# Moving the gates' scratch off the complex scan's buffer, and one product per scan step instead of two

## Chip, cores and metric

The kernel runs on one core of a Trainium2 chip. A core has five engines that matter here: PE (TensorE, matrix multiplications), DVE (VectorE), ACT (ScalarE), POOL (GpSimd) and SP (SyncE, which issues the transfers). Each engine takes its own instructions strictly in the order of its queue, and waits for the others through semaphores. The metric is the device time of one execution in microseconds (us); lower is better.

## What the kernel computes

One layer of a hybrid encoder on 1024 positions of width 1024 in float32: four token mixers in parallel (gated DeltaNet, S5, RG-LRU, a short gated convolution), then cross-attention, then a gated feed-forward part. Two pieces matter. The S5 mixer runs a complex linear recurrence in both directions:

```
h_t = a_t h_{t-1} + b_t
a2r * b1r - a2i * b1i + b2r,   a2r * b1i + a2i * b1r + b2i
```

The gated DeltaNet needs, for every head and position, a gate and a decay, which are small:

```
beta  = sigmoid(beta_logit)
log_a = -exp(a_log) * softplus(alpha + dt_bias)
gam   = cumsum(log_a)            # within chunks
```

## The kernel before

All large products run on PE, each as three products of split float32 parts (`mm3`, L158). PE's instructions stand exactly in the order in which the program is written; the instructions of DVE, ACT, POOL and SP are put in order by a scheduler when the program is built, from its own guess of the times. That order is then fixed.

While the S5 mixer's other work goes on, PE is kept busy by `fill(n)`, which takes the next `n` pieces from a list of projections: a few gate tiles, and then four pairs of RG-LRU and short convolution (`lru`, `short_conv`).

The stage around the change runs like this, all in `tile_trunk` (L1936 to L1951):

- `s5_in` computes the inputs of the recurrence into the buffer `H`. Its last instructions on DVE are the copies at L598.
- `Scalars.run` computes the gates and decays. PE multiplies by a 16-column weight (`mm3` at L764) and transposes the result (L770). Then comes a chain of some seventy small DVE operations of 8 or 64 elements in each of the 128 partitions (`softplus`, `exact_exp`, each operation needs the one before it), with a power taken on POOL in its middle (L721). The result `g` goes back to PE for four small products (L788, L789), which PE issues at a fixed place in its order. DVE picks them up at L792.
- `s5_scan` runs the recurrence on DVE alone: 7 steps of 16 x 64 elements, 15 steps of 64 elements, 7 steps of 15 x 64 elements. A step is `turn` (two cross products into `t1`, one product into `t0`, their sum in `t0`) and an addition into `H`.
- `s5_out`, eight times, reads `H` for the outputs, with `fill(12)` in between. Its first PE instructions need the scan to be done.

The small operations take their scratch from boxes of 1024 columns, in the order in which they ask for it; the first two boxes hold `tri` (L756) and `row` (L765), and everything behind them falls into the third:

```
def part(w):
    if not at or at[-1] + w > S:
        at.append(0)
        self.box = self.big(boxes[len(at) - 1])
...
for go in sc.run(hh, hl, s.parts("xc", "gl", "cm0")):
...
t0, t1 = [self.big(f"cm{i}").rearrange("p (a n) -> p a n", a=16) for i in range(2)]
```

A name such as `cm0` is one buffer. Whoever asks for it again gets it when its last reader is done. The scan's `t0` is `cm0` too. `L` is used by `s5_in` before and by `s5_out` after.

Of the kernel before, what the change touches and what calls it, by code (L numbers as in the profile page):

```python
# [24 lines left out]
ADD, SUB, MUL, MAX, MIN = ALU.add, ALU.subtract, ALU.mult, ALU.max, ALU.min  # L25
# [292 lines left out]
class SPhase:  # L318
# [305 lines left out]
    def s5_scan(self):  # L624

        K = self.K
        H = self.H.rearrange("p (a k) n -> p a k n", k=8)
        t0, t1 = [self.big(f"cm{i}").rearrange("p (a n) -> p a n", a=16) for i in range(2)]

        def turn(out, a, x):  # L630
            n = x.shape[1]
            ri = lambda y: y.rearrange("p n (r g) -> p n r g", r=2)
            b = lambda y: y.unsqueeze(1).to_broadcast([P, n, 64])
            for r in range(2):
                y = slice(32 * r, 32 * r + 32), slice(32 - 32 * r, 64 - 32 * r)
                K.tt(t1[:, :n, y[0]], b(a[1])[:, :, y[0]], x[:, :, y[1]], MUL)
            K.tt(out[:, :n], b(a[0]), x, MUL)
            K.tt(out[:, :n], out[:, :n], t1[:, :n], ADD)

        for k in range(1, 8):  # L640
            turn(t0, self.a8, H[:, :, k - 1])
            K.tt(H[:, :, k], H[:, :, k], t0, ADD)
            yield
        for a in range(1, 16):
            turn(t0, self.a64, H[:, a - 1:a, 7])
            K.tt(H[:, a:a + 1, 7], H[:, a:a + 1, 7], t0[:, 0:1], ADD)
            if a % 5 == 0:
                yield
        for k in range(7):
            turn(t0, self.a8, t0[:, 0:15] if k else H[:, 0:15, 7])  # L650
            K.tt(H[:, 1:16, k], H[:, 1:16, k], t0[:, 0:15], ADD)
            yield
# [539 lines left out]
def gate_tile(K, pool, i, hh, hl):  # L1192
    ps = yield from K.proj(K.a["wi"][GT + i], hh, hl)
    t = pool.tile([P, S], F32, name="tho")
    K.nc.scalar.activation(t, ps, AF.Tanh, scale=0.5)
    K.nc.sync.dma_start(K.th[i], t)
    yield False
# [32 lines left out]
def mem_kv(K, norm):  # L1230

    nc, tc, a = K.nc, K.tc, K.a
    M = 256
    K.kvd = K.dram.tile([16, P, M], F32, name="kvd")
    with tc.tile_pool(name="kv", bufs=1) as p, tc.tile_pool(name="kvr", bufs=2) as r, \
            tc.tile_pool(name="kvw", bufs=5) as w:
        x = p.tile([P, KD, M], F32, name="mx")
        ready = [f() for f in K.weights(a["wkv"][0], pool=w)]
        for k in range(0, KD, 2):
            nc.sync.dma_start(x[:, k:k + 2], a["mem"][:, k:k + 2])  # L1240
        hm = p.tile([P, 2, KD, M], F32R, name="hm")
        acc, row, late = [], None, []
        for k in range(KD):
            K.gained(r, x[:, k], k, "xamn", hm[:, 0], hm[:, 1], acc)
        rr = K.rrow(r, p, acc[0], M)
        steps = (1, 5, 8)
        for i in range(16):
            ps = K.sm.tile([P, 512], F32, name="sm")[:, :M]
            parts = K.weights(a["wkv"][i], pool=w) if i else [lambda x=x: x for x in ready]
            g = K.mm3(ps, parts, hm[:, 0], hm[:, 1], n=M)  # L1250
            if i in (1, 2):
                for _ in range(18):
                    next(g)
                row = next(rr)
            if i in steps:
                next(norm)
            K.run(g)
            late.append((i, ps))
            while late and row is not None:
                j, ps = late.pop(0)  # L1260
                t = r.tile([P, M], F32, name="kvt")
                K.tt(t, ps, row, MUL)
                nc.sync.dma_start(K.kvd[j], t)
# [636 lines left out]
@with_exitstack  # L1900
def tile_trunk(ctx, tc, a, out):
    ctx.enter_context(tc.manual_schedule(engines={mybir.EngineType.PE}))
    K = _K(ctx, tc, a)
    nc = tc.nc
    big = ctx.enter_context(tc.tile_pool(name="big", bufs=1))
    h = big.tile([P, 2, KD, S], F32R, name="big")
    hh, hl = h[:, 0], h[:, 1]
    with tc.tile_pool(name="xin", bufs=2) as xp:
        X = xp.tile([P, KD, S], F32, name="X", bufs=1)

        def norm():
            acc = []
            for k in range(KD):
                nc.sync.dma_start(X[:, k], a["x"][:, k])
                K.sumsq(xp, X[:, k], S, acc)
            yield
            yield from K.normed(xp, lambda k: X[:, k], acc[0], "mixn", hh, hl)

        mem_kv(K, norm())
    K.lo = "dve"  # L1920
    fill = Fill()
    with tc.tile_pool(name="tho", bufs=1, side="right") as tp, ExitStack() as gs:
        gates = [gate_tile(K, tp, i, hh, hl) for i in range(32)]
        sc = Scalars(K, gs)
        with ExitStack() as c:
            s = SPhase(K, c, hh, hl, fill)
            fill.add(*gates[:5])
            for j in range(4):
                fill.add(s.pair(j))
            fill.add(*gates[5:6])  # L1930
            s.s5_prep()
            s.s5_c()
            s.lru_prep()
            for j in range(4):
                s.s5_u(j)
            s.s5_in()  # L1936
            waits = [12, 12, 46, 0]
            scan = s.s5_scan()
            for go in sc.run(hh, hl, s.parts("xc", "gl", "cm0")):
                if not go:  # L1940
                    fill(waits.pop(0))
            K.lo = "pool"
            for _ in scan:
                fill(16)
            fill(12)
            for o in range(8):
                s.s5_out(o)
                fill(12)
            fill(48)
            s.s5_glu()  # L1950
            fill.drain()  # L1951
        K.lo = "pool"
        fill.add(*gates[6:])
        with ExitStack() as c:
            g = GPhase(K, c, hh, hl, fill, sc)
            g.heads()
            fill.drain()
    mg = branches(K, big)
    x1d = K.dram.tile([KD, P, S], F32, name="x1d")
    with tc.tile_pool(name="keep", bufs=1, side="right") as keep, tc.tile_pool(name="bq", bufs=1) as bq:  # L1960
        rcol = keep.tile([P, 8], F32, name="rcol")
        with tc.tile_pool(name="at", bufs=1) as at:
            with tc.tile_pool(name="xr", bufs=1) as xr:
                hx = Quarters(bq)
                kT = at.tile([P, 2, KD, 256], F32R, name="kT")
                vt = at.tile([P, 2, 2, D], F32R, name="vt")
                mem = memory(K, at, kT, vt)
                acc = []
                with tc.tile_pool(name="x1", bufs=1) as xp:
                    for j in range(KD):  # L1970
                        x = xp.tile([P, S], F32, name="X")
                        nc.sync.dma_start(x, a["x"][:, j])
                        ps = K.run(K.proj(a["wmo"][j], mg[:, 0], mg[:, 1]))
                        K.tt(x, x, ps, ADD)
                        for h in range(2):
                            K.scaled(x[:, 512 * h:512 * h + 512], j, "xan", hx.at(0, j, h), hx.at(1, j, h))
                        K.sumsq(xr, x, S, acc)
                        nc.sync.dma_start(x1d[j], x)
                        next(mem)
                qt = big.tile([P, 2, KD, S], F32R, name="big")  # L1980
                es = {}
                rrow = queries(K, xr, hx, qt, acc[0],
                               lambda: es.update({n: scores(K, at, qt, kT, n) for n in range(AHEAD)}), keep, rcol)
            with tc.tile_pool(name="att", bufs=1) as p:
                ot = Quarters(bq)
                tail = Tail(K, tc, bq, keep, rrow, rcol, x1d, out)
                attend(K, p, at, qt, ot, kT, vt, es, tail.ahead)
        tail.run(big, ot)
# [16 lines left out]
```

## Time and profile before

| what | value |
|---|---|
| median of 3 runs | 2454.89 us (2451.81 to 2455.99) |
| the profiled execution, its own time | 2456.03 us |
| its span in the trace | 2454.2 us |
| PE busy | 2360.2 us, 96% of the span |
| DVE busy | 1495.9 us, 61% |
| ACT busy | 927.5 us, 38% |
| POOL busy | 898.4 us, 37% |
| mean granted share of PE's clock | 0.983 |

Busy time is the time in which an engine executes something. An engine that is rarely busy can still set the end, where the busiest one waits for it. The granted clock is the share of PE's full 2.4 GHz that it was given; 0.5 is the lower level of 1.2 GHz.

### The profile page before, as it was taken

To read this page: it belongs to the slowest core of one execution; us is meant where nothing else is said; L and a number is where in the kernel's file an instruction comes from. 1 tells how busy PE (TensorE), PEld (TensorE's weight loads), DVE (VectorE), ACT (ScalarE), POOL (GpSimd) and SP (SyncE) were. 2 spreads that over 40 slices of the span, in tenths; PEclk is the share of its full clock that TensorE was granted. 3 is DMA by queue.
4 is the path that set the end of the run, shared out by engine and by line. 5 is a ranking of instruction groups with operands and counts; after the bars stand their busy time and mean duration, and the time that the engine had idled before them with its cause. 6 is when DMAs were issued, how large, how long until landed. Compare 5 with 4: busy or idle time off the path is not lost. (4 is left out here: it accounts for less than half of the span.)

```text
span 2454.2 us, 31835 instructions
## 1 busy us (share of the span) xinstructions
PE 2360.2 (96%) x11495; PEld 1920.8 (78%) x11495; DVE 1495.9 (61%) x2983; ACT 927.5 (38%) x1461; POOL 898.4 (37%) x644
## 2 busy tenths in 40 slices
PE   7999998899999999999999999999899999999997
PEld 6777767778877787787778888888688888888886
DVE  6883998855947848569345543275766666663421
ACT  6372444634323233232222133255444444453431
POOL 6422224435324233232122222204344444564543
PEclk8999998999999999999899999999999999999998
DMA  7443112342111211112165444105322222255541
GB/s 260 118 109 98 39 65 74 106 146 75 65 48 48 69 48 57 61 53 69 40 235 176 146 153 136 48 5 177 124 77 78 78 78 78 94 180 161 193 157 63
DMA packets 136206, 250.45 MB, mean 102 GB/s; under 512 B 15344, under 2 KB 42992, under 8 KB 135920
## 3 DMA queue, kind: packets, MB, share of 16 engines
q1 hardware_dynamic: 136048, 248.41, 31.2%
q8 instruction: 91, 1.49, 0.2%
q14 instruction: 67, 0.55, 0.1%
HBM read 188.58 MB, written 57.67 MB: 100 GB/s over the span
## 5 line engine op out<-in xcount | busy, mean ns | idle before, releaser
L142 POOL TENSOR_TENSOR wl<-wr,wh 128x512 fp32r<-128x512 f32 (+1 forms) x507 | 695.0, 1380 | 1308.7 <-ACT wh L140 1151.5
L171 PE MATMUL pp<-big,wh 128*128 128x512 f32 x2560 | 729.9, 403 | 16.0 <-DVE sa L192 12.3
L140 ACT ACTIVATE wh<-wr 128x512 fp32r<-128x512 f32 (+1 forms) x526 | 320.2, 621 | 977.2 <-PE pp L171 515.0
L171 PEld LDWEIGHTS pp<-big,wh 128*128 128x128 f32 x2560 | 475.1, 191 | 118.1 <-DVE sa L192 14.6
L171 PE MATMUL pp<-big,wl 128*128 128x512 f32 x1280 | 407.4, 400 | 0.0
L1483 PE MATMUL sm<-big,wh 128*128 128x512 f32 x1096 | 343.8, 395 | 6.0 <-ACT p L1702 4.4
L1483 PE MATMUL sm<-bigq,wh 128*128 128x512 f32 x1008 | 315.6, 394 | 0.7 <-ACT u L1706 0.7
L171 PEld LDWEIGHTS pp<-big,wl 128*128 128x128 f32 x1280 | 238.2, 191 | 47.9
L1483 PEld LDWEIGHTS sm<-big,wh 128*128 128x128 f32 x1096 | 206.3, 188 | 54.2 <-ACT p L1702 4.8
L1483 PEld LDWEIGHTS sm<-bigq,wh 128*128 128x128 f32 x1008 | 189.0, 188 | 45.1 <-ACT u L1706 1.1
L1483 PE MATMUL sm<-big,wl 128*128 128x512 f32 x548 | 214.8, 392 | 0.0
L1483 PE MATMUL sm<-bigq,wl 128*128 128x512 f32 x504 | 197.1, 391 | 0.0
L171 PE MATMUL pp<-yhl,wh 128*128 128x512 f32 x512 | 137.5, 390 | 2.1 <-DVE acc L189 0.8
L1483 PEld LDWEIGHTS sm<-big,wl 128*128 128x128 f32 x548 | 103.4, 189 | 23.2
L189 DVE SCALAR_TENSOR_TENSOR pp<-ut,vec,pp 128x1023 f32<-128x1023 f32 x88 | 113.2, 1286 | 3.5 <-ACT pp L1760 0.4
L171 PEld LDWEIGHTS pp<-yhl,wh 128*128 128x128 f32 x512 | 95.9, 188 | 23.0 <-DVE acc L189 1.2
L1483 PEld LDWEIGHTS sm<-bigq,wl 128*128 128x128 f32 x504 | 94.7, 188 | 21.2
L192 DVE TENSOR_TENSOR t<-rb,x 128x8 f32<-128x8 f32 (+30 forms) x248 | 81.4, 366 | 0.0
L171 PE MATMUL pp<-yhl,wl 128*128 128x512 f32 x256 | 79.0, 390 | 0.0
L192 DVE TENSOR_TENSOR y<-y,t 128x8 f32<-128x8 f32 (+30 forms) x248 | 72.3, 330 | 0.0
L1760 ACT ACTIVATE pp<-ut,vec 128x1024 f32<-128x1024 f32 x44 | 53.1, 1207 | 46.5 <-DVE ut L192 46.5
L171 PE MATMUL pp<-bigq,wh 128*128 128x512 f32 x256 | 69.0, 392 | 0.0
(428 smaller groups left out, 3349.6 us busy)
## 6 DMA issues: line engine op xcount, KB each, us to landing
wr<-in_wi SPq DMA_DIRECT2D x144, 256.0 KB, 2.7
wr<-in_wup SPq DMA_DIRECT2D x88, 256.0 KB, 4.2
wr<-in_wdn SPq DMA_DIRECT2D x80, 256.0 KB, 3.9
thd<-tho SPq DMA_DIRECT2D x32, 512.0 KB, 2.9
thi<-thd SPq DMA_DIRECT2D x32, 512.0 KB, 4.1
gd<-sg SPq DMA_DIRECT2D x22, 512.0 KB, 2.9
gr<-gd SPq DMA_DIRECT2D x44, 256.0 KB, 4.1
wr<-in_wkv SPq DMA_DIRECT2D x32, 256.0 KB, 3.6
```

Of the source, the lines that this page charges most:

```text
L140: self.nc.scalar.activation(hi, src, AF.Copy)
L142: e.tensor_tensor(lo, src, hi.bitcast(F32), SUB)
L171: self.nc.tensor.matmul(ps[:, o:o + step], w[:, i], r[:, k, o:o + step], start=first, stop=last)
L189: self.nc.vector.scalar_tensor_tensor(out, in0, s, in1, op0, op1)
L192: (eng or self.nc.vector).tensor_tensor(out, a, b, op)
L1483: self.K.nc.tensor.matmul(ps, a[:, i], b, start=start and i == 0 and j == 0, stop=last and stop is not False, skip_group_check=stop is Non ...
L1760: K.nc.scalar.activation(c[b], t[b], AF.Identity, bias=K.v("fconvb", n), scale=K.v("fconv", 3 * n + 1))
```

## The change

Two edits. The third box of the small operations is `L` in place of `cm0`. And the two cross products of a scan step, each over half of the 64 columns, become one over all of them, which reads the halves of `x` in reversed order.

```diff
@@ s5_scan
             ri = lambda y: y.rearrange("p n (r g) -> p n r g", r=2)
             b = lambda y: y.unsqueeze(1).to_broadcast([P, n, 64])
-            for r in range(2):
-                y = slice(32 * r, 32 * r + 32), slice(32 - 32 * r, 64 - 32 * r)
-                K.tt(t1[:, :n, y[0]], b(a[1])[:, :, y[0]], x[:, :, y[1]], MUL)
+            K.tt(ri(t1[:, :n]), ri(b(a[1])), ri(x)[:, :, ::-1], MUL)
             K.tt(out[:, :n], b(a[0]), x, MUL)
@@ tile_trunk
-            for go in sc.run(hh, hl, s.parts("xc", "gl", "cm0")):
+            for go in sc.run(hh, hl, s.parts("xc", "gl", "L")):
```

Lines behind the first edit stand two lower in the changed kernel (L792 is L790 there).

PE's order is the same in both, row by row, but for the name of the buffer that L788 and L789 read. What moves is the order of DVE, and with it that of ACT, POOL and SP. The names end in a buffer number here: `cm0_2283` and `L_2283` are the small operations' scratch, `cm0_2502` and `cm1_2503` the scan's `t0` and `t1`, `a80` and `a81` the two parts of a factor, `sm_2480` the result of L788 and L789.

On DVE, before, at the end of the small operations and the start of the scan:

```order
L192 TENSOR_TENSOR cm0_2283<-cm0_2283 128x64
L189 SCALAR_TENSOR_TENSOR cm0_2283<-cm0_2283 128x64
L192 TENSOR_TENSOR cm0_2283<-cm0_2283 128x64
L792 COPY cm0_2283<-sm_2480 128x64
...
L192 TENSOR_TENSOR cm0_2502<-a80_908,H_903 128x1024
L192 TENSOR_TENSOR g_kd_2486<-g_kd_2486,g_beta_2282 128x64
L192 TENSOR_TENSOR cm0_2502<-cm0_2502,cm1_2503 128x1024
L192 TENSOR_TENSOR H_903<-H_903,cm0_2502 128x16x64
L192 TENSOR_TENSOR cm1_2503<-a81_909,H_903 128x16x32 x2
```

The first use of `t0` stands behind the last use of the scratch, so all but two products of the scan come after L792.

On DVE, after, directly behind the last copy of `s5_in` into `H`:

```order
L598 COPY H_903<-sm_2078 64x4x128
L192 TENSOR_TENSOR cm1_2503<-a81_909,H_903 128x1024
L192 TENSOR_TENSOR cm0_2502<-a80_908,H_903 128x1024
L192 TENSOR_TENSOR cm0_2502<-cm0_2502,cm1_2503 128x1024
L192 TENSOR_TENSOR H_903<-H_903,cm0_2502 128x16x64
...
L199 TENSOR_SCALAR L_2283<-vec_71 128x8
L192 TENSOR_TENSOR cm0_2502<-cm0_2502,cm1_2503 128x1024
L197 TENSOR_SCALAR L_2283<-L_2283 128x8
```

The scan now begins at once, and the small operations stand singly between its rows, from its second step on.

On DVE, after, at the end of the small operations:

```order
L192 TENSOR_TENSOR cm0_2502<-cm0_2502,cm1_2503 128x960
L189 SCALAR_TENSOR_TENSOR L_2283<-L_2283 128x64
L192 TENSOR_TENSOR H_903<-H_903,cm0_2502 128x15x64
L192 TENSOR_TENSOR cm1_3428<-apc0_906,s5p_901 128x512
L192 TENSOR_TENSOR L_2283<-L_2283 128x64
...
L790 COPY L_2283<-sm_2480 128x64
```

The last small operation, the product that gives `g`, now stands behind the last row of the whole scan and behind a first product of `s5_out` (`cm1_3428`).

## Rows read from the trace of the kernel before

**Rows 1.** The page's first part: busy time, share of the span, instructions.

```profile
PE 2360.2 (96%) x11495; PEld 1920.8 (78%) x11495; DVE 1495.9 (61%) x2983; ACT 927.5 (38%) x1461; POOL 898.4 (37%) x644
```

**Rows 2.** Timeline of PE: start, length, engine, instruction, [idle before <-releaser].

```profile
242.81 0.30 PE L788 MATMUL sm<-cm,xc 128*128 128x32 f32 x2
...
297.37 2.08 PE L171 MATMUL pp<-big,wh 128*128 128x512 f32 x4 [4.42 <-DVE sa L192]
...
369.29 2.08 PE L171 MATMUL pp<-big,wh 128*128 128x512 f32 x4 [6.03 <-DVE sa L192]
...
399.99 0.46 PE L675 MATMUL sm<-L,wt 128*128 128x128 f32 x2 [1.33 <-DVE wt L192]
...
412.26 0.61 PE L675 MATMUL sm<-L,wt 128*128 128x128 f32 x2 [3.89 <-DVE L L671]
```

**Rows 3.** Busy time by stretch: its length, PE, PEld, DVE, ACT, POOL, clock, DMA.

```profile
242.80:390.00 147.20, 134.90 (x541) 104.35 (x540) 138.21 (x189) 60.07 (x65) 38.87 (x23) 0.95 0.17 56
390.00:500.00 110.00, 97.16 (x488) 79.92 (x487) 91.69 (x105) 59.24 (x63) 53.74 (x44) 0.97 0.37 106
296.40:303.20 6.80, 5.83 (x14) 4.58 (x15) 6.45 (x16) 4.63 (x4) 0.00 (x0) 0.50 0.04 14
368.10:374.90 6.80, 5.61 (x13) 4.46 (x14) 6.80 (x9) 3.52 (x3) 0.00 (x0) 0.50 0.00 0
412.50:419.20 6.70, 5.85 (x25) 5.39 (x25) 3.58 (x5) 0.71 (x1) 1.12 (x4) 0.50 0.47 110
```

**Rows 4.** Timeline of DVE from the last copy into H to the gates.

```profile
190.45 1.08 DVE L598 COPY H<-sm 64x512 f32<-64x512 f32 x1
...
214.28 0.69 DVE L142 TENSOR_TENSOR wl<-wr,wh 128x512 fp32r<-128x512 f32 x1 [19.14 <-ACT wh L140]
216.72 0.20 DVE L199 TENSOR_SCALAR g_beta<-g_beta 128x64 f32<-128x64 f32 x1 [1.76 <-ACT g_beta L776]
```

**Rows 5.** Timeline of DVE in the first and the second stretch of the scan.

```profile
252.13 1.23 DVE L192 TENSOR_TENSOR cm<-cm,cm 128x1024 f32<-128x1024 f32 x1
253.39 1.23 DVE L192 TENSOR_TENSOR H<-H,cm 128x1024 f32<-128x1024 f32 x1
...
323.29 0.23 DVE L192 TENSOR_TENSOR cm<-cm,cm 128x64 f32<-128x64 f32 x1
323.55 0.23 DVE L192 TENSOR_TENSOR H<-H,cm 128x64 f32<-128x64 f32 x1
```

**Rows 6.** Timeline of DVE in the scan's third stretch.

```profile
368.02 1.22 DVE L192 TENSOR_TENSOR sa<-pp,sa 128x1024 f32<-128x1024 f32 x1
369.15 1.15 DVE L192 TENSOR_TENSOR H<-H,cm 128x960 f32<-128x960 f32 x1
370.22 1.22 DVE L192 TENSOR_TENSOR cm<-a,cm 128x480 f32<-128x480 f32 x2
```

**Rows 7.** Timeline of DVE: small operations, dependent (219) and independent (244).

```profile
219.17 0.20 DVE L197 TENSOR_SCALAR cm<-cm 128x64 f32<-128x64 f32 x1
219.40 0.23 DVE L192 TENSOR_TENSOR cm<-cm 128x64 f32<-128x64 f32 x1
...
244.19 0.19 DVE L795 CAST g_gh<-cm 128x64 fp32r<-128x64 f32 x1
244.29 0.22 DVE L192 TENSOR_TENSOR g_kd<-sm,cm 128x64 f32<-128x64 f32 x1
```

**Rows 8.** Timeline of DVE: three products of a scan step, twice.

```profile
248.57 3.52 DVE L192 TENSOR_TENSOR cm<-a,H 128x512 f32<-128x512 f32 x3
...
269.74 2.43 DVE L192 TENSOR_TENSOR cm<-a,H 128x512 f32<-128x512 f32 x3
```

**Rows 9.** Timeline of POOL: the power, and a split.

```profile
223.03 10.55 POOL L721 TENSOR_TENSOR cm<-cm 128x64 f32<-128x64 f32 x1 [24.21 <-DVE cm L720]
...
248.74 1.67 POOL L142 TENSOR_TENSOR wl<-wr,wh 128x512 fp32r<-128x512 f32 x1 [5.11 <-ACT wh L140]
```

**Rows 10.** Timeline of DVE while POOL takes the power.

```profile
225.99 0.69 DVE L142 TENSOR_TENSOR wl<-wr,wh 128x512 fp32r<-128x512 f32 x1 [3.11 <-ACT wh L140]
```

## Prediction, made before the changed kernel was run

> **What bounds the kernel now.** I read the page's busy times first: PE is busy 96% of the span [rows 1], and its order is the same before and after, so a change can move the end only by making PE idle more or less, or by changing its clock. So next the timeline of PE around the changed stage. Up to L788, the products that need the gates' chain, PE arrives at 242.81 and does not wait [rows 2]: the chain was ready. Behind it PE waits for DVE four times for long: 4.42 and 6.03 us for `sa` (the short convolution's first product), 1.33 us for `wt` and 3.89 us for `L` (both for the first two rounds of `s5_out`) [rows 2], together 15.7 us. The stretches by clock show what follows each long wait: three stretches of 6.7 to 6.8 us at a granted clock of 0.50, that is 1.2 GHz [rows 3]. Half of each is lost, 3.4 us, together 10.2 us.
>
> Then the timeline of DVE, to see why it is late there. It is done with `H` at 190.45 + 1.08 = 191.5, and then does nearly nothing: one idle stretch alone is 19.14 us, up to the split at 214.28 [rows 4]. The scan's `t0` shares `cm0` with the chain's scratch and has to wait until the chain is through. From 242.8 to 390 it is the reverse: DVE is busy 138.21 of 147.20 us [rows 3], because the scan and four directions of the RG-LRU compete; `sa` starts only at 368.02 [rows 6], and PE waits for it until 369.29. So before, DVE is idle ahead of the chain and late behind it.
>
> **The change, part by part.** With `L` as scratch, nothing holds `t0`, and the scan moves into the idle stretch. But a queue is served in order. The last operation of the gates' chain now stands behind the last row of the scan, and PE stands at L788 (L786 after) until it is done. So the question is when DVE gets through the scan.
>
> *Prices on DVE.* An operation that needs the one before it starts 0.03 us after that one's end: 252.13 to 253.39 is 1.26 for a length of 1.23, 323.29 to 323.55 is 0.26 for 0.23 [rows 5]. One that does not need it starts some 0.08 us before the other's end: 368.02 to 369.15 is 1.13 for 1.22, and 369.15 to 370.22 is 1.07 for 1.15 [rows 6]; small independent ones start 0.10 apart, 244.19 to 244.29 [rows 7].
>
> *The scan.* A step now has two products that don't need each other, a sum, and the addition into `H`. First stretch: 1.14 + 3 x 1.26 = 4.92, seven times 34.4 us. Second: 0.10 + 3 x 0.26 = 0.88, fifteen times 13.2 us. Third, where the next step needs the sum and not `H`: 2 x 1.07 + 2 x 1.18 = 4.50, seven times 31.5 us. Together 79.1 us.
>
> *The merged product* saves two starts where one remains: 2 x 0.6 against 1.14 in a large step, one start of 0.10 in a small one, some 2.3 us in all, already in the sum. The trace has no such form, with halves in reversed order. Lower bound: the length of any product of 1024 elements, 1.23 [rows 5]. Upper: the copy at L598, which writes `H` backwards and column by column, takes 1.08 for 512 elements [rows 4], which would make 2.2 of 1.23 and 14 x 0.95 = 13.3 us more. I take the lower, since the innermost 32 columns still run forward, as in the old halves.
>
> *What else stands in DVE's queue up to the chain's end.* Five splits of weights of 0.69 (0.6 from start to start): 3.0 us. One product of `s5_out`: 0.6 us. 66 small operations of the chain: where one stands between a scan operation and the one that needs it, it is hidden (1.13 + 0.10 is less than 1.26); elsewhere it costs 0.10 [rows 7]. I take half of them, 3.3 us; bounds 0 and 66 x 0.23 = 15.2 us, the spacing of dependent ones (219.17 to 219.40 [rows 7]). The chain waits for PE and ACT once, for `g_beta` at 216.72 [rows 4]; by the prices above DVE gets to that row at about 216.4, so this costs 0.3, which I leave out.
>
> *POOL.* The power takes 10.55 us [rows 9] and lies beside ten steps of the second stretch, 9.9 us with what stands between: 0.7 us remain. A POOL operation of 512 columns beside the scan costs DVE about 1.1 us: three products take 3.52 us when POOL splits weights at 248.74, against 2.43 [rows 8, 9]. Two splits and one product of POOL fall into the new stretch: 3.3 us.
>
> **A rule on POOL's cost**: the Trainium skill (SBUF — State Buffer, Who interferes with whom) says that the port pair shared by DVE and GpSimd is an exclusive lock, held for a whole instruction. For the split the trace agrees roughly (1.1 of 1.67 us). For the power it does not: a DVE split with two inputs at 225.99 takes 0.69, inside the 10.55 us of the power [rows 9, 10]. By the rule the power would shut DVE out; that is a rival below.
>
> *Sum.* The chain ends at 191.5 + 79.1 + 3.0 + 0.6 + 3.3 + 0.7 + 3.3 = 281.5. PE stands from 242.8 on: a new wait of 38.7 us. Behind it comes a stretch at half clock, as behind each wait of about 4 us and more: 3.4 us (bounds 0 and two such stretches, 6.8). While PE stands, nothing is gained elsewhere: ACT and POOL can prepare only the three buffers of weights that there are.
>
> *What is given back.* When PE goes on, the scan is done, DVE has only the RG-LRU and the short convolution, and `s5_out`'s first inputs can be made at once. So the four waits (15.7 us) and the three half-clock stretches (10.2 us) go: 25.9 us. The small waits inside `s5_out` stay, since its own copies set them. Bounds: 18 us, if one of the `sa` waits stays with its slow stretch, and 35.3 us, if all of PE's idle time from 242.8 to 500 goes (147.20 - 134.90 and 110.00 - 97.16 [rows 3] are 25.1, with the 10.2).
>
> Net: 38.7 + 3.4 - 25.9 = +16.2 us. The profiled execution took 2456.03 us, its span 2454.2: 2472.2 for the change against it. Its time was 1.1 above the median, so I predict 2471 us, 0.7% slower.
>
> **Rivals.**
>
> *All is given back.* The chain's small operations cost nothing, POOL's don't disturb: the chain ends at 191.5 + 79.1 + 3.6 = 274.2, the wait is 31.4, with the slow stretch 34.8, and all 35.3 us behind are repaid: -0.5, 2454 us. It decides where the chain ends before about 275. For it: DVE's load behind the scan falls by more than half. Against it: waits for ACT and for `s5_out`'s own copies are among the 25.1. Faster than before needs still more: DVE rows that are shorter than any of their form here.
>
> *The small operations cost their full length.* 66 x 0.23 in place of 3.3: +11.9, 2483 us. Against it stand the starts 0.10 apart [rows 7]. The Trainium skill has this as a rule: VectorE: DVE Perf Modes, The DRAIN you can't avoid, says that the next operation does not start until the pipe is empty, though it lets one that is not held start earlier. By the rule the time would be those 2483 us; the trace disagrees, with 0.10 between starts of operations that last 0.19 and 0.22.
>
> *POOL's power shuts DVE out:* the ten steps it was to cover come behind it, +9.9 us, 2481 us; against it the split of 0.69 [rows 10].
>
> *The reversed product is slow:* +13.3 and a little for the small steps, 2485 us; nothing in the trace is nearer to it than the forward products.
>
> *The scan does not start early,* since something else holds it: then the time would be the old one. The order shows no such thing; the first scratch row in `L` must wait for transfers out of `L`, but stands behind six scan rows.
>
> **How the numbers follow.** A measurement of this kernel tells about 0.2% (4.9 us) from no change. Chances: my forecast (2462 to 2479) 0.69; the three ways in which DVE is slower (2479 to 2490) 0.21 together; all given back, or the scan not early, 0.07 (no change that can be told); rows shorter than any of their form, 0.03 (faster). The first two add up to slower, 0.90. The range from 2461 to 2486 leaves out the cases near the old time and the sum of two slow ones.
>
> **What the new profile would show.** Right: one wait of PE at L786 for DVE's `L`, about 39 us, ending near 281; DVE without idle time from 191 on, apart from a short one for POOL's power; the last addition into `H` just ahead of that, where before it came behind the addition at 369.15 [rows 6]; no wait for `sa` above 1 us behind it, and no half-clock stretches but the one behind the long wait; small operations 0.10 apart; the merged product at 1.2 and 0.22 us. Wrong: if PE's wait is much shorter than 30 us, my price of the scan is wrong; if it is above 50, the small operations or the merged product cost more; if `sa` still makes PE wait, the scan was not what delayed it.

## The result, and the profile after

| | before | changed |
|---|---|---|
| median of 4 runs each | 2455.03 us (2451.81 to 2455.99) | 2475.27 us (2471.36 to 2475.96) |
| ratio, 95% interval | | 1.0072 [1.0059, 1.0084] |
| span of the profiled execution | 2454.2 us | 2473.2 us |

The change makes the kernel 0.72% slower by the ratio on record; the two medians alone stand 20.2 us, 0.82%, apart. 2471 us were predicted. The medians of the kernel before lay between 2457 and 2459 us in the later sessions, so versions are compared below by their ratio to the kernel before in the same session.

The page's first part after; it answers to [rows 1]:

```profile
PE 2355.2 (95%) x11495; PEld 1916.1 (77%) x11495; DVE 1476.7 (60%) x2954; ACT 927.3 (37%) x1461; POOL 886.6 (36%) x644
```

Nothing shows in these sums: every engine does the same work or a little less. The loss is waiting, so the timeline of PE from 242 to 500 us is next; these are its waits above 1 us, in the columns of [rows 2]:

```profile
283.99 0.64 PE L786 MATMUL sm<-L,xc 128*128 128x32 f32 x2 [41.34 <-DVE L L192]
...
442.20 1.21 PE L171 MATMUL pp<-big,wh 128*128 128x512 f32 x4 [1.38 <-ACT gl L394]
...
462.08 1.19 PE L171 MATMUL pp<-big,wh 128*128 128x512 f32 x4 [1.13 <-ACT sa L348]
```

One wait of 41.34 us stands where before there was none, and none of the four long waits of [rows 2] is left. Busy time by stretch, in the columns of [rows 3]; the third stretch is the one that was granted half the clock:

```profile
242.80:390.00 147.20, 104.15 (x428) 81.66 (x429) 83.91 (x108) 49.88 (x54) 36.05 (x25) 0.85 0.13 45
390.00:500.00 110.00, 105.04 (x533) 85.62 (x533) 83.36 (x97) 61.62 (x64) 40.44 (x41) 1.00 0.34 97
244.65:289.02 44.37, 5.03 (x16) 4.35 (x17) 43.61 (x65) 0.19 (x1) 10.19 (x7) 0.50 0.04 16
```

DVE has 83.91 us to do between 242.8 and 390, where it had 138.21: it is ahead. The clock was at 0.50 through nearly all of the wait and until 5.03 us of work had been done behind it, and then at full speed; the three slow stretches of [rows 3] are gone.

DVE's timeline, its corner points:

```profile
190.42 2.36 DVE L192 TENSOR_TENSOR cm<-a,H 128x1024 f32<-128x1024 f32 x2
...
213.94 0.69 DVE L142 TENSOR_TENSOR wl<-wr,wh 128x512 fp32r<-128x512 f32 x1 [0.94 <-ACT wh L140]
...
216.38 0.20 DVE L199 TENSOR_SCALAR g_beta<-g_beta 128x64 f32<-128x64 f32 x1 [0.54 <-ACT g_beta L774]
...
229.56 0.23 DVE L192 TENSOR_TENSOR cm<-a,H 128x64 f32<-128x64 f32 x1
231.11 0.69 DVE L142 TENSOR_TENSOR wl<-wr,wh 128x512 fp32r<-128x512 f32 x1 [1.32 <-ACT wh L140]
...
236.61 0.36 DVE L192 TENSOR_TENSOR cm<-a,H 128x64 f32<-128x64 f32 x2
...
237.52 0.36 DVE L192 TENSOR_TENSOR cm<-a,H 128x64 f32<-128x64 f32 x2
...
246.10 1.27 DVE L192 TENSOR_TENSOR L<-L 128x64 f32<-128x64 f32 x1 [0.66 <-POOL L L719]
247.29 1.30 DVE L192 TENSOR_TENSOR H<-H,cm 128x64 f32<-128x64 f32 x1
248.51 1.15 DVE L192 TENSOR_TENSOR cm<-a,H 128x960 f32<-128x960 f32 x1
...
261.67 1.16 DVE L192 TENSOR_TENSOR H<-H,cm 128x960 f32<-128x960 f32 x1
262.74 1.15 DVE L192 TENSOR_TENSOR cm<-a,cm 128x960 f32<-128x960 f32 x1
263.81 0.22 DVE L192 TENSOR_TENSOR L<-L 128x64 f32<-128x64 f32 x1
263.95 1.15 DVE L192 TENSOR_TENSOR cm<-a,cm 128x960 f32<-128x960 f32 x1
...
280.33 1.15 DVE L192 TENSOR_TENSOR H<-H,cm 128x960 f32<-128x960 f32 x1
281.40 1.54 DVE L192 TENSOR_TENSOR cm<-apc,s5p 128x512 f32<-128x512 f32 x1
282.87 1.07 DVE L192 TENSOR_TENSOR L<-L 128x64 f32<-128x64 f32 x1
```

The scan runs from 190.42 to 281.48 without a long break. The last small operation, 282.87, stands behind the last addition into `H`, 280.33; it ends at 283.94, and PE goes on at 283.99. POOL, in the same stretch:

```profile
235.51 10.55 POOL L719 TENSOR_TENSOR L<-L 128x64 f32<-128x64 f32 x1 [4.49 <-DVE H L192]
246.03 2.48 POOL L142 TENSOR_TENSOR wl<-wr,wh 128x512 fp32r<-128x512 f32 x2
```

### The profile page after: what moved, and what is told of

It reads as the page before. It is cut to its first block, busy times and chain, and to the rows that moved or that the text cites. A ratio compares the mean times of both kernels' runs of the same rounds, so it can differ in the third digit from the quotient of the medians.

```text
span 2473.2 us, 31808 instructions
## 1 busy us (share of the span) xinstructions
PE 2355.2 (95%) x11495; PEld 1916.1 (77%) x11495; DVE 1476.7 (60%) x2954; ACT 927.3 (37%) x1461; POOL 886.6 (36%) x644
## 5 line engine op out<-in xcount | busy, mean ns | idle before, releaser
L142 POOL TENSOR_TENSOR wl<-wr,wh 128x512 fp32r<-128x512 f32 (+1 forms) x507 | 684.3, 1359 | 1302.0 <-ACT wh L140 1147.9
```

Source lines behind the costliest of these rows:

```text
L142: e.tensor_tensor(lo, src, hi.bitcast(F32), SUB)
```

## The experiments

My theory at first: the scratch alone makes the wait, since it lets the scan go ahead of the small operations in DVE's queue; the merged product only shortens the scan. The rivals: the merged product costs time itself, or PE waits for something else.

### The two edits apart

The scratch alone:

```diff
-            for go in sc.run(hh, hl, s.parts("xc", "gl", "cm0")):
+            for go in sc.run(hh, hl, s.parts("xc", "gl", "L")):
```

> The scratch of the small operations in L, the two cross products of a scan step kept apart. Theory (the scratch alone makes the new wait, the merged product only shortens the scan): PE waits for the last small operation until 2 to 3 us later than in the changed kernel, so for about 43 to 44 us in place of 41.3; 2476 to 2479 us. Rival (the merged product with its reversed halves is what costs time): no wait of tens of us, time within 5 us of 2455.

The product alone:

```diff
-            for r in range(2):
-                y = slice(32 * r, 32 * r + 32), slice(32 - 32 * r, 64 - 32 * r)
-                K.tt(t1[:, :n, y[0]], b(a[1])[:, :, y[0]], x[:, :, y[1]], MUL)
+            K.tt(ri(t1[:, :n]), ri(b(a[1])), ri(x)[:, :, ::-1], MUL)
```

> The merged product alone, the small operations' scratch stays in the scan's own buffer. Theory: the scan stays behind the small operations, no new wait; DVE saves some 2.3 us over the scan, so the later waits for sa and L shrink by up to that: 2452 to 2455 us. Rival (the merged product costs time): 2460 us or more.

| version | time, before in the same session | ratio, 95% interval |
|---|---|---|
| scratch alone | 2460.39, 2459.17 us | 1.0012 [1.0002, 1.0022] |
| product alone | 2452.56, 2459.17 us | 0.9976 [0.9967, 0.9986] |

Both theories missed the scratch alone. Its loss is 0.12%, not the 0.8% or more of the first. But it does have a wait of tens of microseconds, which the rival excluded. The timeline of PE in this version, and of DVE ahead of it:

```profile
268.81 0.63 PE L788 MATMUL sm<-L,xc 128*128 128x32 f32 x2 [25.30 <-DVE L L192]
```

```profile
264.99 1.16 DVE L192 TENSOR_TENSOR H<-H,cm 128x960 f32<-128x960 f32 x1
...
268.54 0.22 DVE L192 TENSOR_TENSOR L<-L 128x64 f32<-128x64 f32 x1
268.67 1.16 DVE L192 TENSOR_TENSOR cm<-cm,cm 128x960 f32<-128x960 f32 x1
```

264.99 is the third of the seven additions of the scan's third stretch. So with two products per step the last small operation stands behind three of these steps, and with the merged product it stands behind all seven. PE's wait is 25.30 us in place of 41.34.

The product alone gains 0.24%, some 6 us, more than the 0 to 3 us expected, and shows that the merged operation costs nothing of its own there. Where the next part of the layer begins, with its first product on `vtok`, the profile of this version is 3.0 us ahead of that before (713.3 and 716.3, the first starts in the rows below), as expected; the rest of its gain arises behind that, and what makes it was not followed:

```profile
L1106 PE MATMUL sm<-vtok,Y x16: 272/275/275, 713.3 to 1197.2; 128*128 128x128 f32 x16
L1108 PE MATMUL sm<-vtok,Y x16: 272/276/276, 716.3 to 1202.9; 128*128 128x128 f32 x16
```

The effects don't add up: -0.24% and +0.12% would give -0.12%, and together they give +0.72%. So the first theory falls in the part on the merged product. The new one: what counts is behind how many scan steps the last small operation stands in DVE's order, and the merged product moved it back, since a step with fewer rows leaves fewer places at which a small operation can stand. The traces bear out the last part: from the second step of the third stretch on, one small operation stands behind each row of a step but the addition, four to a step with two cross products and three with one. Why the scheduler places them so is not shown.

### The place of the last small operation

Three versions of the changed kernel move that place. In the first two, the cross products are kept apart in one stretch of the scan alone (`n == 15` is the third, `n == 1` the second):

```diff
-            K.tt(ri(t1[:, :n]), ri(b(a[1])), ri(x)[:, :, ::-1], MUL)
+            if n == 15:
+                for r in range(2):
+                    y = slice(32 * r, 32 * r + 32), slice(32 - 32 * r, 64 - 32 * r)
+                    K.tt(t1[:, :n, y[0]], b(a[1])[:, :, y[0]], x[:, :, y[1]], MUL)
+            else:
+                K.tt(ri(t1[:, :n]), ri(b(a[1])), ri(x)[:, :, ::-1], MUL)
```

> The changed kernel, with the two cross products kept apart in the third stretch of the scan alone (merged in the first two). Theory now (what counts is behind how many scan steps the last small operation stands in DVE's order, and the merged product moved it from behind 3 of the third stretch's 7 steps to behind all 7, since a step with fewer rows takes in fewer small operations): here it stands behind 5 of 7, so PE's wait is some 9 us shorter than 41.3, about 32 us, and the time some 8 to 9 us below the changed kernel's, a ratio to the kernel before near 1.0037 (1.002 to 1.005). Rival (the reversed product itself holds DVE up, wherever it is used): the third stretch has none, so the wait is about 25 us as with two products everywhere, and the ratio about 1.001.

> The changed kernel, with the two cross products kept apart in the second stretch alone (15 small steps). Theory: the last small operation stands behind 5 of the 7 steps here too, so the wait is about 32 us and the ratio near 1.0037 (1.002 to 1.005). Rival (the reversed product itself holds DVE up): only the small steps are spared, some 1.5 us, so the wait stays at 39 us or more and the ratio at 1.0065 or more.

In the last, all operations keep their form, and the third stretch has to wait for the small operations, because its `t0` is in their buffer:

```diff
+        t0 = self.big("L").rearrange("p (a n) -> p a n", a=16)
         for k in range(7):
             turn(t0, self.a8, t0[:, 0:15] if k else H[:, 0:15, 7])
```

> The changed kernel, but the whole third stretch of the scan has its t0 in L, and so has to wait until the small operations are done. No operation of DVE has another form; only the place of the last small operation changes, which stands ahead of all 7 steps of the third stretch. Theory (place in the order): the small operations behind POOL's power take 8 to 11 us, so PE waits 11 to 15 us in place of 41.3; some of the gain goes back, since the third stretch's 31 us now compete with RG-LRU: ratio 0.995 to 1.000. Rival (the small operations, or POOL's power ahead of them, are late in themselves): PE's wait stays above 25 us, ratio above 1.002.

PE's wait in the three versions, in this order:

```profile
276.22 0.63 PE L791 MATMUL sm<-L,xc 128*128 128x32 f32 x2 [33.05 <-DVE L L192]
```

```profile
276.33 0.64 PE L791 MATMUL sm<-L,xc 128*128 128x32 f32 x2 [33.50 <-DVE L L192]
```

```profile
259.54 0.63 PE L787 MATMUL sm<-L,xc 128*128 128x32 f32 x2 [15.85 <-DVE L L192]
...
316.30 1.20 PE L171 MATMUL pp<-big,wh 128*128 128x512 f32 x4 [3.25 <-DVE sa L192]
```

| version | steps of the third stretch ahead | PE's wait | ratio, 95% interval |
|---|---|---|---|
| third stretch held | 0 of 7 | 15.85 us | 0.9985 [0.9976, 0.9994] |
| scratch alone | 3 of 7 | 25.30 us | 1.0012 [1.0002, 1.0022] |
| two products in the third | 5 of 7 | 33.05 us | 1.0031 [1.0020, 1.0043] |
| two products in the second | 5 of 7 | 33.50 us | 1.0042 [1.0028, 1.0056] |
| the change | 7 of 7 | 41.34 us | 1.0072 [1.0059, 1.0084] |

Wait and time follow the place, whichever stretch has the merged product, and the two versions with two products in one stretch waited as forecast (about 32 us). The rivals fall: with two products in the third stretch the wait is not 25 us, with two in the second it is not 39, and with every operation in its form and only the order changed it is 15.85, a little above the 11 to 15 us forecast. A wait that is 25.5 us shorter there is worth 0.87%, 21 us; the rest goes back to the third stretch, which now competes with RG-LRU (a wait of 3.25 us for `sa` has returned).

### Does PE have other work for that time?

44 pieces of `fill` are moved ahead of the waiting products, and taken from those behind:

```diff
                 if not go:
                     fill(waits.pop(0))
+                    if len(waits) == 1:
+                        K.lo = "pool"
+                        fill(44)
             K.lo = "pool"
+            moved = 44
             for _ in scan:
-                fill(16)
+                fill(16 - min(moved, 16))
+                moved -= min(moved, 16)
```

> The changed kernel, with 44 of the 272 pieces of projections that PE does during the scan put ahead of the products that wait (46 there become 90), nothing else. Theory (PE has work, but its order puts the waiting products too early): PE reaches them at about 283 and waits little; the 41.3 us and the 2.5 us of slow clock behind are saved, and what was repaid stays repaid: 2431 to 2440 us. Rival (DVE's work is only pushed along: with PE working on, RG-LRU and short convolution compete with the scan again and the waits for sa return): 2447 to 2456 us.

2466.23 us against 2459.17, ratio 1.0029 [1.0020, 1.0038]: less than half of the gain that the theory wanted, and above the rival's range too. The timeline of PE, and of DVE:

```profile
287.47 0.64 PE L786 MATMUL sm<-L,xc 128*128 128x32 f32 x2 [24.78 <-DVE L L192]
...
298.08 2.90 PE L403 MATMUL pp<-xc,lw 128*128 128x512 f32 x3 [6.83 <-DVE xc L189]
```

```profile
289.15 3.01 DVE L192 TENSOR_TENSOR cm<-apc,s5p 128x512 f32<-128x512 f32 x2
292.08 0.21 DVE L790 COPY L<-sm 128x64 f32<-128x64 f32 x1
292.21 1.27 DVE L189 SCALAR_TENSOR_TENSOR xc<-pp,vec,xc 128x1022 f32<-128x1022 f32 x1
```

I had taken the pieces for twice as long as they are: the wait now begins at 287.47 - 24.78 = 262.69, so 44 pieces filled 20 us. The small operations end later too: PE's products begin at 287.47, 3.5 us later than in the changed kernel. And directly behind them PE needs `xc`, whose operations stand behind the scan, the small operations and rows of `s5_out` in the same queue of DVE. So moving so much is not a way out: PE's work from there on hangs on the queue that is late. Both theories were right in part: the wait is 16.6 us shorter, and 6.83 us have returned elsewhere.

### The scan in two parts

The place can also be set by hand. From a chosen step of the first stretch on, the scan's `t0` is in `L`, so that it waits for the small operations; the steps before that run in DVE's idle stretch. Four steps early, and five (`k == 6`), and three (`k == 4`):

```diff
         for k in range(1, 8):
+            if k == 5:
+                t0 = self.big("L").rearrange("p (a n) -> p a n", a=16)
             turn(t0, self.a8, H[:, :, k - 1])
```

> The changed kernel, but from its fifth step on the scan's t0 is in L, where it has to wait for the small operations to be done. So four steps run in the idle stretch, then the small operations run without the scan between them. Theory (the wait of PE comes from the small operations standing behind the scan, the gain from DVE being early): PE waits for them under 4 us; the scan is about 22 us less late than before, so most of the 25.9 us of waits and slow clock behind is repaid: 2430 to 2442 us. Rival (small operations are late for another reason, such as the buffer L or POOL): PE still waits 10 us or more, above 2450 us.

> As the version with the scan in two parts, but five steps in place of four run ahead of the small operations. Theory: the fifth step (5 us) fits into the idle time ahead of the gates' first row, the small operations still end before PE comes to them, and the later wait of 3.96 us for sa with its slow clock goes: 1 to 6 us below the version with four, a ratio to the kernel before of 0.989 to 0.991. Rival (the fifth step makes the small operations late): PE waits 2 us or more for them, ratio 0.992 or more.

> As the version with the scan in two parts, but three steps in place of four run ahead of the small operations. Theory (the later waits follow from how late the scan is): PE does not wait for the small operations, as with four; the rest of the scan is 5 us longer, so the later waits and slow clock grow by 0 to 6 us: ratio 0.991 to 0.994. Rival (four steps already hold the small operations up somewhere, as five do): three are faster than four, ratio below 0.990.

Five steps early with 12 pieces moved (as above, with 12 for 44), and four steps early with two products everywhere:

> Five steps ahead of the small operations, as in the version that waits 4.50 us for them, and 12 pieces of projections (some 5.4 us of PE) moved ahead of the waiting products, taken from those behind. Theory (the 4.50 us and the slow clock behind it are all that the fifth step costs there): PE comes to the products when they are ready, and 4.5 to 6 us are saved against the version with five, ratio 0.9947 to 0.9957. Rival (the moved pieces only bring PE sooner to work that waits for DVE): under 2 us saved, ratio above 0.9962.

> The version with the scan in two parts (four steps early), with the two cross products kept apart everywhere. Theory (the merged product harms only through the place of the last small operation, which is ahead of the scan's second part here in either case): the merged product is worth its saving alone, so the time without it is 2 to 6 us above that with it, a ratio to the kernel before of 0.992 to 0.994. Rival (the merged product costs something of its own in this stage): the time without it is below, ratio under 0.990.

| version | time, before in the same session | ratio, 95% interval |
|---|---|---|
| three steps early | 2441.00, 2458.20 us | 0.9934 [0.9918, 0.9950] |
| four steps early | 2438.19, 2459.17 us | 0.9914 [0.9899, 0.9928] |
| four, two products | 2440.76, 2457.09 us | 0.9927 [0.9904, 0.9951] |
| five steps early | 2450.12, 2457.70 us | 0.9972 [0.9960, 0.9983] |
| five, 12 pieces moved | 2440.94, 2458.20 us | 0.9926 [0.9908, 0.9945] |

Four steps early have the lowest ratio, 0.86% below the kernel before, within what was expected and clearly below the change. The intervals of three steps, of two products and of five steps with moved pieces overlap with it, so no order among these four is shown; five steps without moved pieces are clearly slower. Three steps came out as their theory had it, 0.991 to 0.994. The timelines of PE and of DVE with four steps:

```profile
243.45 0.30 PE L788 MATMUL sm<-L,xc 128*128 128x32 f32 x2
...
297.56 2.07 PE L171 MATMUL pp<-big,wh 128*128 128x512 f32 x4 [3.96 <-DVE sa L192]
```

```profile
211.41 1.23 DVE L192 TENSOR_TENSOR cm<-a,H 128x1024 f32<-128x1024 f32 x1
...
241.41 0.22 DVE L192 TENSOR_TENSOR L<-L 128x64 f32<-128x64 f32 x1
...
245.42 1.23 DVE L192 TENSOR_TENSOR L<-a,H 128x1024 f32<-128x1024 f32 x1
```

The small operations end at 241.63, 1.8 us before PE comes to L788, and only then does the rest of the scan begin, but for one merged product at 211.41, which does not need `t0`. Of the waits of [rows 2] one of 3.96 us is left. Five steps use up the 1.8 us and more, as that run's rival had it. PE and DVE of that version:

```profile
246.93 0.63 PE L788 MATMUL sm<-L,xc 128*128 128x32 f32 x2 [4.50 <-DVE L L192]
...
303.84 2.08 PE L171 MATMUL pp<-big,wh 128*128 128x512 f32 x4 [4.48 <-DVE sa L192]
...
347.72 2.07 PE L171 MATMUL pp<-big,wh 128*128 128x512 f32 x4 [3.30 <-ACT gl L394]
```

```profile
238.86 1.30 DVE L192 TENSOR_TENSOR L<-L 128x64 f32<-128x64 f32 x1 [7.28 <-POOL L L721]
```

The fifth step makes the small operations late ahead of POOL's power, so that the power, too, starts and ends 4.2 us later. POOL with four steps early, and with five:

```profile
224.09 10.55 POOL L721 TENSOR_TENSOR L<-L 128x64 f32<-128x64 f32 x1 [3.02 <-DVE L L720]
```

```profile
228.27 10.55 POOL L721 TENSOR_TENSOR L<-L 128x64 f32<-128x64 f32 x1 [2.27 <-DVE L L720]
```

With 12 pieces moved there, no wait is left at L788, and 0.46%, some 11 us, are saved, about twice what I expected: besides the 4.50 us, the wait of 3.30 us for `gl` and two of the three slow stretches behind L788 are gone. Here moved pieces do help; the small operations were only 4.5 us late. Whether the merged product is worth its saving in the version with four steps stays open: the ratio is lower with it, as expected, but the intervals overlap; only a cost of its own so large that the time without it fell below 0.990 is excluded.

## Why the prediction was right, step by step

**The mechanism.** PE waits at L786 for the last small operation, which stands behind the whole scan: shown by the rows at 283.99 and 282.87, and by the versions that move the place alone.

**The wait, 38.7 us predicted, 41.34 measured.** DVE needed from 190.42 to 283.94, 93.5 us, where the sum had 79.1 + 3.0 + 0.6 + 3.3 + 0.7 + 3.3 = 90.0. By stretches: 190.42 to 229.56 is 39.1 us: seven steps of 4.92, four splits of 0.6, 1.5 of waits for ACT, and 0.8 for small operations. 229.56 to 248.51 is 19.0: 13.2 for the steps, a split, 2.0 of waits, 1.9 more for two operations that lie beside POOL's splits, and 1.2 for small operations. 248.51 to 281.40 is 32.9: 31.5 and 1.4. Behind that 2.5: the product, the small operation, and 1.7 of contention with POOL. So the small operations cost about 3.6 us (3.3 predicted), the contention 3.6 (3.3), and the wait for the power 0.66 (0.7). What the sum left out is 2.8 us of waits for ACT (0.94, 0.54 and 1.32 in the rows): splits of weights, and the gates' `g_beta`, that stand ahead of scan rows and are not ready yet. I had counted 0.3 and left it out. The step on DVE's queue failed there: I asked what a row costs, and not for each row of another job whether its input is there. The scan also began 1.1 us sooner than the 191.5 of the sum, which hid part of this: the chain ended 2.4 us later than forecast.

**The slow stretch behind the wait, 3.4 us predicted:** half of the 5.03 us of work in it, 2.5. The 3.4 was half of a stretch's length; but PE also idled in those stretches and worked for 5.83, 5.61 and 5.85 us [rows 3], so that by the same measure each had cost 2.8 to 2.9 us.

**What is given back, 25.9 us predicted.** The four waits and the three slow stretches are gone, and between the long wait and 733 us none above 1.38 us is left. The first product with `vtok` of the next part began at 716.3 us before and at 733.0 after (the first start below), 16.7 later; 41.34 + 2.5 - 16.7 = 27.1 us were given back up to there.

```profile
L1106 PE MATMUL sm<-vtok,Y x16: 272/275/275, 733.0 to 1219.6; 128*128 128x128 f32 x16
```

Both terms of the 25.9 were off, one each way. The three slow stretches had cost half of 17.3 us of work, 8.6 and not 10.2. And the prediction's four waits were not all: before, PE also waited for DVE here, both times longer than the 1.33 us that was counted:

```profile
467.92 1.20 PE L171 MATMUL pp<-big,wh 128*128 128x512 f32 x4 [1.89 <-DVE sa L192]
...
485.95 1.20 PE L171 MATMUL pp<-big,wh 128*128 128x512 f32 x4 [1.77 <-DVE sb L192]
```

From 242.8 to 500 PE idled for 25.1 us before and for 48.0 after, 41.2 of them in the new wait, by the stretches above; so about 18 us of waits were given back, and not 15.7.

**The net, 16.2 us predicted.** Up to `vtok` it is 16.7. That this is so near is in part luck: the wait was 2.6 us longer than forecast, the slow stretch 0.9 shorter, and 1.2 more were given back. The spans differ by 19.0; most of the other 2.3 us come around 1634 us, where the changed kernel's profile has a short stretch at half clock and that of before has none (half of 3.41 is 1.7). What makes that stretch I did not follow.

```profile
1633.87:1637.28 3.41, 3.41 (x17) 3.31 (x17) 2.42 (x10) 1.29 (x7) 0.00 (x0) 0.50 0.00 0
```

**The merged product, 2.3 us saved.** By itself that is nearly right: the products of a large step take 2.36 us in place of 2.43 [rows 8], and the merged product alone makes the kernel faster, not slower. But I took DVE's order as given from the built kernel and put the blame for it on the scratch. The scratch alone costs 0.12%; the larger part of the loss comes when the merged product, on top of the scratch, moves the last small operation back. The time came out right because the order was read from the changed kernel, not because the edits were rightly weighed.

**The rivals.** Not all was given back. Small operations do not cost their full length: with one between two products they start 263.95 - 262.74 = 1.21 apart, and 262.74 - 261.67 = 1.07 without one, 0.14 for an operation of 0.22. The Trainium skill's rule (VectorE: DVE Perf Modes, The DRAIN you can't avoid) that the next operation waits until the pipe is empty would ask for the 0.22; these rows disagree with it, as those of before did, and agree with the page's exception, that an operation which is not held starts earlier. POOL's power does not shut DVE out: inside it, 235.51 to 246.06, a scan step takes 237.52 - 236.61 = 0.91 us, with its four operations in it. The reversed product is not slow. The scan did start early.

**The signs.** Most of those that the prediction named are there. Three were off: DVE also stood idle for ACT three times; PE waits 1.13 us for `sa` at 462.08, though for ACT and not for DVE; and small operations lie 0.14 us apart among the large rows, not 0.10.

## What to carry to other kernels

Freeing a buffer removes a wait, but also an order: what the wait held back may now stand ahead of something short that the bounding engine needs, in a queue that is served strictly in turn. So look up where the last operation of the short chain stands in the built order, and let a long job with time to spare start early only as far as it ends before that chain has to run (here three or four of the first stretch's seven steps). And an edit that saves rows on such an engine can move other rows: measure two edits apart and together.

## What the runs showed of the hardware

- Beside POOL's splits an operation of DVE with 64 elements per partition takes 1.27 and 1.30 us in place of 0.23 (246.10 and 247.29, beside 246.03 + 2.48 on POOL): each was held for about 1.0 us, where the three products of 512 elements in [rows 8] took 1.1 us more in all. POOL's power of 10.55 us held no short operation for long: a scan step beside it took 0.91 us (236.61 to 237.52).
- Reversing two halves of 32 columns in the input costs DVE nothing that shows: 1.23 us for the one that reverses, by itself (211.41, four steps early), as for the forward operations of 1024 elements in [rows 5]; 2.36 us for both products of a step.
- PE's granted clock was 0.50 from 244.65, some 2 us after it had fallen idle, to 289.02, 5.0 us after it went on, at the end of an idle time of 41.34 us; around the ends of waits of 4 to 6 us it was 0.50 for 6.7 to 6.8 us, with 5.6 to 5.9 us of work in them [rows 3]. In the version with the product alone, behind a wait of 4.61 us, it was 0.50 from 298.65 to 302.05, with 3.26 us of work. So the clock cost 2.5 us behind the longest wait, and 1.6 to 2.9 behind these short ones: in these traces the cost does not follow the length of the wait.
